# A fifth Strassen pair in the gate and up blocks of an encoder layer, and weights streamed from one array in load order

## The chip, the cores and the metric

The kernel runs on one core of one Trainium2 chip. TensorE (PE) multiplies into PSUM banks; VectorE (DVE), ScalarE (ACT) and GpSimd (POOL) prepare its operands and take its results; SyncE (SP) issues the loads, and 16 DMA engines carry all transfers. The metric is the device time of one execution in microseconds, the median of three runs. A profile is one further execution with its own time. Everything is computed in float32; a product of full precision is made of three matmuls of a faster rounded format (fp32r), as told below.

## The reference, cut to what matters

One layer over 256 rows of width 2048. An input projection of 5120 columns feeds differential attention and a convolution group; both are concatenated and go through an output projection. The part that the change touches is the second half, a gated feed-forward network with 5632 hidden columns:

```
h  = h + einsum('bsm,md->bsd', mixed, w_out)
hn = rms_norm(h, norm2_g)
a  = einsum('bsd,df->bsf', hn, w_gate)
bu = einsum('bsd,df->bsf', hn, w_up)
h  = h + einsum('bsf,fd->bsd', silu(a) * bu, w_down)
```

All weights, some 51 million float32 numbers, are read once from memory.

## The kernel before, in words

*Chunks.* The work of TensorE is a list of chunks, built ahead and run in that order by `run_chunks` (line 411). An ordinary chunk, called a "two" here, is a piece of a weight matrix of two row blocks of 128 by 512 columns. Each is cut in two parts on the chip: `hi`, its rounding to fp32r (`round_chunk`, line 328, on ScalarE, written to tile `whi`), and `lo`, the residue (`split_chunk`, line 336, on VectorE, tile `wlo`). The activations are cut the same way. A product is then hi·hi + lo·hi + hi·lo: three matmuls with 512 columns for each row block and each of the two halves (m = 0, 1) of the 256 rows, 12 for a two.

*Residues by DMA.* For some twos (`by_dma`) ScalarE writes -raw to `wlo` (line 333) behind the rounding, and GpSimd issues a DMA that adds raw's rounding to it in place (line 334), so that VectorE has nothing to do for it. `BY_DMA`, `DOWN_BY_DMA` and `gate_up_block` choose which.

*Pairs.* The 256 rows are two halves, gate and up are two column blocks, and two row blocks of 128 of the weights can be taken together: a 2x2 by 2x2 product. A "pair" (kind `s`) computes it with seven products in place of eight (`PRODUCTS`), so 21 matmuls where four row blocks as twos (one two of gate, one of up) take 24. It costs sums: of the activations once (`make_forms`, line 985, before the first block; `make_down_forms`, line 939, for each down pass), and for each pair of the weights: `first_sums` (lines 1035 to 1037) makes four sums (tile `wt`) from the loaded four pieces (tile `wb`, three of which are also used as they are); `round_pair` and `split_pair` round all seven on ScalarE (lines 1030 and 1052, tile `wh`) and take seven residues on VectorE (line 1059, tiles `wlb` and `wlt`).

*Blocks.* The feed-forward network has 11 blocks of 512 gate and 512 up columns (j = 0 to 10), in groups of 4, 4 and 3, each group followed by a down pass of two blocks. A block's order is a string: `s` a pair, `g` a two of gate, `u` a two of up (`ORDER`, `ORDERS`). Before, a block has pairs for the row blocks 0 to 3 with 8 to 11, and four twos each of gate and up for the rest (`REST`, `TWOS`). Behind its last pair, `bank_sums` (line 1183) combines the banks on VectorE with six sums and calls `sums_aside` (line 1039), in which GpSimd makes the first sums of the next pair that is not yet rounded, if it is loaded; `products_done` applies silu on ScalarE (lines 1202 and 1203); `block_done` (line 1206) takes two sums and two products on VectorE after the block's last two; `transposed` (line 893) transposes the result on TensorE for the down pass. The operand sums of a down pass are made during the last blocks of its group, one step at a time (`lag`).

*What sets the order.* The engines' instructions are issued in one fixed order by this program. While chunk t is multiplied, the residues of chunk t+2 and the rounding of chunk t+3 are issued (`LO_AHEAD`, `HI_AHEAD`), and everything that hangs on a finished chunk is a generator that advances at each `resume()`, two to a two and four to a pair. Each engine takes its own instructions strictly in that order, and a wait holds all behind it. `whi` and `wlo` have three buffers, `wh`, `wlb`, `wlt` and `wb` two, `wt` one, the loaded raw pieces `RAW_BUFS`; loads are issued on SP when a buffer is given up (`load_freed`).

*The passage to the network.* `out_done` (line 836) adds each quarter of the output projection to h, transposes it on TensorE (`ps_h`), scales it and cuts it, and sums its squares. The residual h is stored to memory (`hd`) by GpSimd's DMAs, and the down passes add to it there.

## Time and profile before

| | us |
|---|---|
| median of three runs (lowest, highest) | 1034.13 (1034.05, 1034.5) |
| the profiled execution, in all | 1035.56 |
| its span, first to last instruction | 1033.8 |
| TensorE busy | 1023.9 |
| VectorE busy | 906.9 |
| ScalarE busy | 668.0 |
| GpSimd busy | 179.6 |

The input projection with attention and convolution takes the first 247 us or so, the output projection goes to 338.7, where the first chunk of the feed-forward network starts, and the network fills the rest. The granted clock of TensorE was 1.00 in all windows shown. Matmuls are pipelined: a row gives 0.39 us for a single one, but the next starts before it ends, so that start to start is the cost that counts; for VectorE too, an instruction's row is a little longer than the step to the next one. A row of the timeline holds the start, the length, the engine, the line, the operation, output and inputs, shapes and the count, and in brackets the idle time before it with what ended it.

### The profile page before, as it was taken

What the parts mean: (1) busy time and instruction counts of PE and PEld (TensorE: products, weight loads), DVE (VectorE), ACT (ScalarE), POOL (GpSimd) and SP (SyncE); (2) the same over time, 40 slices, a digit from 0 to 9 for tenths busy, and PEclk for the clock granted to TensorE, in tenths of its full rate; (3) what the DMA queues carried; (4) which work ended last, traced back from release to release, by engine and by line L of the source; (5) the groups of instructions that cost most, each with busy time, mean ns of one, the idle gap of its engine ahead of it and who ended that gap; (6) DMA issues with size and microseconds to landing.
All of it is one profiled execution on the core that took longest, in us unless ns stands there. A gap on an engine that the chain in (4) does not pass through costs nothing.

```text
span 1033.8 us, 13146 instructions
## 1 busy us (share of the span) xinstructions
PE 1023.9 (99%) x4628; PEld 846.3 (82%) x4628; DVE 906.9 (88%) x1163; ACT 668.0 (65%) x863; POOL 179.6 (17%) x190
## 2 busy tenths in 40 slices
PE   9999999999999899999999999999999999999998
PEld 7888888888888688888888888888888888888887
DVE  6899999999756999899988897889989888789897
ACT  7644656665756576777756657677777556767662
POOL 0300112110000100212203222123022231220320
PEclk9999999999999999999999999999999999999999
DMA  9757554445458767987989898889798989797776
GB/s 339 248 198 260 187 184 164 160 167 171 164 175 278 221 220 218 285 261 210 255 256 230 292 276 252 254 240 240 245 280 236 260 231 302 228 259 229 234 190 176
DMA packets 116738, 239.71 MB, mean 232 GB/s; under 512 B 7872, under 2 KB 9152, under 8 KB 116672
## 3 DMA queue, kind: packets, MB, share of 16 engines
q1 hardware_dynamic: 105216, 203.58, 58.7%
q0 software_dynamic: 11168, 35.13, 18.1%
q8 instruction: 36, 0.59, 0.2%
q14 instruction: 30, 0.25, 0.1%
q10 hardware_dynamic: 288, 0.16, 0.1%
HBM read 204.24 MB, written 9.44 MB: 207 GB/s over the span
## 4 chain that ended last, share of the span: by engine, by line
PE 92%; DMA 3%; DVE 2%; issue 2%; ACT 0%; SPq 0%; POOL 0%; DVEq 0%; POOLq 0%; ACTq 0%
PE q L1102 11%; PE q L1096 11%; PE q L1097 11%; PE q L1077 9%; PE q L1076 9%; PE q L1075 9%; PE acc L369 9%; PE acc L370 9%; PE acc L375 9%; DMA wlo<-raw 2%; PE ps_a L903 1%; DVE wlo L339 1%; DMA raw<-in_w_in_dram 1%; PE ps_s L726 1%; PE ps_o L796 1%
## 5 line engine op out<-in xcount | busy, mean ns | idle before, releaser
L330 ACT CAST whi<-raw 128x1024 fp32r<-128x1024 f32 (+1 forms) x248 | 257.4, 1044 | 192.1 <-issue 87.5
L339 DVE TENSOR_TENSOR wlo<-raw,whi 128x1024 fp32r<-128x1024 f32 (+1 forms) x198 | 238.4, 1211 | 47.1 <-ACT whi L330 42.8
L1059 DVE TENSOR_TENSOR wlt<-wt,wh 128x1024 fp32r<-128x1024 f32 x130 | 153.1, 1219 | 16.4 <-ACT wh L1052 16.4
L1052 ACT CAST wh<-wt 128x1024 fp32r<-128x1024 f32 x130 | 132.6, 1051 | 36.2 <-DVE wt L1035 24.3
L1096 PE MATMUL q<-whi,chi 128*128 128x512 f32 x352 | 137.8, 391 | 0.0
L1097 PE MATMUL q<-whi,clo 128*128 128x512 f32 x352 | 137.0, 389 | 0.0
L1059 DVE TENSOR_TENSOR wlb<-wb,wh 128x1536 fp32r<-128x1536 f32 x65 | 113.9, 1753 | 16.2 <-ACT wh L1030 16.2
L334 POOL DMA_DIRECT2D wlo<-raw x50 | 43.6, 871 | 484.3 <-ACT wlo L333 313.9
L369 PE MATMUL acc<-whi,xhi 128*128 128x512 f32 x312 | 124.1, 398 | 0.0
L370 PE MATMUL acc<-whi,xlo 128*128 128x512 f32 x312 | 122.0, 391 | 0.0
L1075 PE MATMUL q<-wh,fhi 128*128 128x512 f32 x308 | 120.6, 392 | 0.0
L1076 PE MATMUL q<-wh,flo 128*128 128x512 f32 x308 | 119.9, 389 | 0.0
L1030 ACT CAST wh<-wb 128x1536 fp32r<-128x1536 f32 x65 | 95.8, 1473 | 8.9 <-PE q L1076 3.3
L586 DVE SCALAR_TENSOR_TENSOR y<-upad,cw,y 128x256 f32<-128x256 f32 x240 | 100.9, 480 | 0.0
L1102 PE MATMUL q<-wlo,chi 128*128 128x512 f32 x352 | 94.6, 390 | 3.2 <-DMA wlo<-raw 2.5
L375 PE MATMUL acc<-wlo,xhi 128*128 128x512 f32 x312 | 85.0, 393 | 0.0
L1102 PEld LDWEIGHTS q<-wlo,chi 128*128 128x128 f32 x352 | 65.8, 188 | 17.9 <-DMA wlo<-raw 3.5
L1096 PEld LDWEIGHTS q<-whi,chi 128*128 128x128 f32 x352 | 66.1, 188 | 13.6
L1097 PEld LDWEIGHTS q<-whi,clo 128*128 128x128 f32 x352 | 66.1, 188 | 13.5
L1096 PE MATMUL q<-whi,ahi 128*128 128x512 f32 x182 | 71.0, 390 | 0.0
L1097 PE MATMUL q<-whi,alo 128*128 128x512 f32 x182 | 70.8, 389 | 0.0
L1077 PE MATMUL q<-wlt,fhi 128*128 128x512 f32 x176 | 68.6, 390 | 0.2 <-DVE wlt L1059 0.2
(247 smaller groups left out, 1844.4 us busy)
## 6 DMA issues: line engine op xcount, KB each, us to landing
raw<-in_w_in_dram SPq DMA_DIRECT2D x78, 512.0 KB, 4.7
wlo<-raw POOLq DMA_DIRECT2D x50, 512.0 KB, 6.3
raw<-in_w_down_dram SPq DMA_DIRECT2D x46, 512.0 KB, 6.2
wb<-in_w_up_dram SPq DMA_DIRECT2D x44, 512.0 KB, 4.4
wb<-in_w_gate_dram SPq DMA_DIRECT2D x44, 512.0 KB, 5.5
raw<-in_w_gate_dram SPq DMA_DIRECT2D x44, 512.0 KB, 5.3
raw<-in_w_up_dram SPq DMA_DIRECT2D x44, 512.0 KB, 5.5
wb<-in_w_down_dram SPq DMA_DIRECT2D x42, 512.0 KB, 5.8
```

Source lines behind the costliest of these rows:

```text
L330: act.copy(c["hi"], c["raw"])
L339: dve.tensor_tensor(c["lo"], c["raw"], c["hi"].bitcast(F32), ALU.subtract)
L369: pe.matmul(ps[m], xhi[:, ms], hi[:, j, :], start=c["first"] and j == 0, stop=False)
L370: pe.matmul(ps[m], xlo[:, ms], hi[:, j, :], start=False, stop=False)
L375: pe.matmul(ps[m], xhi[:, ms], lo[:, j, :], start=False, stop=c["last"] and j == nk - 1)
L1059: dve.tensor_tensor(lo, raw, h.bitcast(F32), ALU.subtract)
L1075: pe.matmul(ps, hi, c["hi"][:, w], start=bool(first), stop=False)
L1076: pe.matmul(ps, lo, c["hi"][:, w], start=False, stop=False)
L1077: pe.matmul(ps, hi, c["lo"][w], start=False, stop=bool(last))
L1096: pe.matmul(ps, xs[i][0][:, ms], hi[:, i, :], start=i == 0 and bool(c["first"].get(qs[m])), stop=False)
L1097: pe.matmul(ps, xs[i][1][:, ms], hi[:, i, :], start=False, stop=False)
L1102: pe.matmul(sum_bank(c, qs[m]), xs[i][0][:, ms], lo[:, i, :], start=False, stop=i == 1 and bool(c["last"].get(qs[m])))
```

## The change

The weights are concatenated by the host into one flat array, in the order of the loads (`Stream`): each load takes the next piece, laid out with a partition's data side by side. A two's load is then a run of 4 KB for each of the 128 partitions (2 x 2 KB before), a pair's is one DMA with runs of 8 KB (two DMAs, 4 x 2 KB before).

Blocks 1 to 10 get a fifth pair, of the row blocks 4 and 5, in place of one two of gate and one of up; the rest is three twos each. Block 0 keeps four pairs, so the rows 4 and 5 are prepared in both forms. The orders become shorter, `sgsgsgsusuu` in place of `sggsggsuusuu`. The twos whose residue goes by DMA are others: gate's second and third and up's first and second (before: gate's first and second, up's second and fourth); in block 1 gate's third and up's first two; in the first block of the second and third group up's first two alone; in the down passes of four blocks, gate's third and fourth for the first and second.

The very first pair's sums go from VectorE to GpSimd and are issued six chunks ahead in place of three, and its loads nine ahead in place of seven. In `out_done` the sums of squares of the last quarter come behind the transposes, its store stays ahead. The operand forms get 640 columns in place of 512 each. The raw buffers go from five to four, with a fifth that lives until the network starts.

```
-RAW_BUFS = 5
+RAW_BUFS = 4
...
-NS = 4
-REST = [k for k in range(KD) if k % HK >= NS]
+PAIRS = [(0, 8), (1, 9), (2, 10), (3, 11), (4, 5)]
+NS = len(PAIRS)
+REST = [k for k in range(KD) if not any(k in p for p in PAIRS)]
 TWOS = [tuple(REST[i : i + 2]) for i in range(0, len(REST), 2)]
-BY_DMA = dict(g=TWOS[:2], u=TWOS[1::2])
-
-ORDER = "sggsggsuusuu"
-ORDERS = {0: "gugusgsgssuu", 1: "gsggsgsuusuu"}
+BY_DMA = dict(g=TWOS[1:], u=TWOS[:2])
+
+ORDER = "sgsgsgsusuu"
+ORDERS = {1: "gsgsgssusuu"}
+
+NS0 = 4
+TWOS0 = [*PAIRS[NS0:], *TWOS]
+ORDER0 = "gugusgsgssuu"
+DOWN_ORDER = "sggsggsuusuu"
...
-DORDERS = {4: (ORDER, ORDER), 3: ("gguusggsuu", "gsgsgsuuu")}
+DORDERS = {4: (DOWN_ORDER, DOWN_ORDER), 3: ("gguusggsuu", "gsgsgsuuu")}
 HD_LAG = 3
-DOWN_BY_DMA = {4: (dict(g=(0, 1), u=(1,)),) * 2, 3: (dict(g=(), u=()), dict(g=(0, 1), u=()))}
+DOWN_BY_DMA = {4: (dict(g=(2, 3), u=(1,)),) * 2, 3: (dict(g=(), u=()), dict(g=(0, 1), u=()))}
...
-PAIRS_AHEAD, SUMS_AHEAD = 7, 3
+PAIRS_AHEAD, SUMS_AHEAD = 9, 6
...
+class Stream:
...
+    def take(self, parts):
+
+        n = P * sum(w for *_, w in parts)
+        self.parts.append(parts)
+        self.at += n
+        return self.ap[self.at - n : self.at].rearrange("(p n) -> p n", p=P)
...
-            sp.dma_start(out=c["raw"][:, :, o : o + n], in_=rows[:, c["rows"], col : col + n])
-            o += n
+        sp.dma_start(out=c["raw"].rearrange("p k n -> p (k n)"),
+                     in_=stream.take([(c["w"], k, col, n) for k in c["ks"] for col, n in c["cols"]]))
...
             if t == first - SUMS_AHEAD:
-                first_sums(chunks[pairs[0]], dve)
+                first_sums(chunks[pairs[0]], pool)
...
         if n == D // N - 1:
-            h_squares(n, cs)
-            yield
-            yield
-            ss = small.tile([P, NM], F32, tag="ssh", name="ssh")
...
+            h_store(cs)
+            yield
+        yield
...
+        h_squares(n, cs)
         if n < D // N - 1:
-            h_squares(n, cs)
+            h_store(cs)
...
-        for i, kind in enumerate("ug"):
-            w, col = c["from"][kind]
-            sp.dma_start(out=c["b"][:, 2 * i : 2 * i + 2, :],
-                         in_=w.rearrange("(k p) n -> p k n", p=P)[:, c["rows"], col : col + N])
+        sp.dma_start(out=c["b"].rearrange("p a n -> p (a n)"),
+                     in_=stream.take([(c["from"][i][0], k, c["from"][i][1], N) for i in "ug" for k in c["ks"]]))
...
-                   BY_DMA if j > 1 and j not in FIRSTS else dict(g=(), u=BY_DMA["u"]) if j else
-                   dict(g=TWOS[2:3], u=TWOS[2:3]), swap=not j)
+                   dict(BY_DMA, g=TWOS[2:]) if j == 1 else BY_DMA if j > 1 and j not in FIRSTS else dict(BY_DMA, g=()) if j else
+                   dict(g=TWOS0[2:3], u=TWOS0[2:3]), swap=not j)
...
+    for c in [c for c in chunks if not c.get("spare_raw")][RAW_BUFS :: RAW_BUFS + 1]:
+        c["kept_raw"] = True
```

More of the change, by code (lines that the diff above doesn't have):

```diff
@@ L310, in block @@
                                first=part[0] == ks[0] and first, last=last and i == len(ks),
-                               done=done if i == len(ks) else None, spare=spare, by_dma=False,
-                               rows=slice(part[0], part[-1] + 1), load=load_chunk, round=round_chunk,
+                               done=done if i == len(ks) else None, spare=spare, by_dma=False, load=load_chunk, round=round_chunk,
                                split=split_chunk, multiply=multiply))
@@ L317, in load_chunk @@
         c["view"] = view
-        if c.get("spare_raw"):
+        if c.get("kept_raw"):
+            c["raw"] = view(keep.tile([P, NK * N], F32, tag="raw", name="raw"))
+        elif c.get("spare_raw"):
             c["raw"] = view(early.tile([P, 4 * N], F32, tag="wb", name="raw")[:, : NK * N])
@@ L414, in run_chunks @@
         pairs = [k for k in range(n) if chunks[k].get("kind") == "s"]
-        raws = [k for k in range(n) if chunks[k].get("kind") != "s" and not chunks[k].get("spare_raw")]
+        raws = [k for k in range(n) if chunks[k].get("kind") != "s" and not (chunks[k].get("spare_raw") or chunks[k].get("kept_raw"))]
         loaded, split = set(), set()
@@ L829, in tile_block, with h_store @@
     rstd2 = [rstd2s[:, m : m + 1] for m in range(NM)]
+    def h_store(cs):
+        for m in range(NM):
+            pool.dma_start(out=hd[m][:, cs], in_=h[m][:, cs])
     def h_squares(n, cs):
@@ L864, in out_done @@
                     pe.transpose(pt[:, i, m * P : (m + 1) * P], h[m][:, (k + i) * P : (k + i + 1) * P], ident)
-            if k % HK < NS:
-                rows = ffn["rows"][:, k // HK, k % HK : k % HK + 2, :]
+            if k not in REST:
                 for i in range(2):
-                    act.activation(rows[:, i, :], pt[:, i, :], AF.Copy, scale=col("g2", k + i))
-            else:
-                a = REST.index(k)
-                hi, lo = (ffn[x][:, a : a + 2, :] for x in ("chi", "clo"))
+                    p, half = next((p, pair.index(k + i)) for p, pair in enumerate(PAIRS) if k + i in pair)
+                    act.activation(ffn["rows"][:, half, p, :], pt[:, i, :], AF.Copy, scale=col("g2", k + i))
+            if k in REST or k in PAIRS[NS0]:
+                a = REST.index(k) if k in REST else 0
+                hi, lo = (ffn[x][:, a : a + 2, :] for x in ("chi", "clo")) if k in REST else lhs_two("h", k)
                 for i in range(2):
@@ L884, in out_done @@
         if n == D // N - 1:
+            yield
+            ss = small.tile([P, NM], F32, tag="ssh", name="ssh")
+            for m in range(NM):
+                dve.tensor_reduce(ss[:, m : m + 1], ss2[m], AX.X, ALU.add)
+            rsqrt_mean(rstd2s, ss, D, EPS)
             keepstack.close()
@@ L991, in make_forms @@
         flo = fp.tile([P, 7, NS, P], F32R, tag="flo", name="flo")
-        f = fp.tile([P, 7, NS, P], F32, tag="wh", name="sums", bufs=2)
-        dve.scalar_tensor_tensor(f[:, 4], a21, -1.0, a22, ALU.mult, ALU.subtract)
-        dve.scalar_tensor_tensor(f[:, 5], f[:, 4], -1.0, a11, ALU.mult, ALU.subtract)
+        f = dict(zip((2, 4, 5, 6), range(4)))
+        f_ = fp.tile([P, 4, NS, P], F32, tag="wh", name="sums", bufs=2)
+        f = {form: f_[:, i] for form, i in f.items()}
+        dve.scalar_tensor_tensor(f[4], a21, -1.0, a22, ALU.mult, ALU.subtract)
+        dve.scalar_tensor_tensor(f[5], f[4], -1.0, a11, ALU.mult, ALU.subtract)
         act.copy(fhi[:, 0], a11)
@@ L1068, in multiply_pair @@
     def multiply_pair(c):
-        while (fs := c["pairs"]()) is None or len(plain) < len(REST):
+        while (fs := c["pairs"]()) is None or len(plain) < len(REST) + 2 * (NS - NS0):
             resume()
@@ L1137, in fast_block @@
             what = left[kind].pop(0)
-            c = dict(kind=kind, sums=sums, swap=swap, done=None, first={}, last={}, rows=what["rows"], **operands)
+            c = dict(kind=kind, sums=sums, swap=swap, done=None, first={}, last={}, ks=what["ks"], **operands)
             if kind == "s":
@@ L1157, in gate_up_block @@
     def gate_up_block(j):
-        fast_block(ORDERS.get(j, ORDER), [dict(p=p, rows=slice(p, p + HK + 1, HK)) for p in range(NS)],
-                   [dict(ks=ks, rows=slice(ks[0], ks[1] + 1, ks[1] - ks[0]), k=ks) for ks in TWOS],
+        fast_block(ORDERS.get(j, ORDER) if j else ORDER0,
+                   [dict(p=p, ks=k) for p, k in enumerate(PAIRS[: NS if j else NS0])],
+                   [dict(ks=ks, k=ks) for ks in (TWOS if j else TWOS0)],
                    dict(g=(w_gate, j * N), u=(w_up, j * N)),
@@ L1174, in down_pass @@
             end = {}
-            fast_block(order, [dict(p=p, rows=slice(k0 + p, k0 + p + HD + 1, HD)) for p in range(nd)], twos,
+            fast_block(order, [dict(p=p, ks=(k0 + p, k0 + p + HD)) for p in range(nd)], twos,
                        dict(g=(w_down, n * N), u=(w_down, (n + 1) * N)),
@@ L1363 @@
     given["rope"] = rope_constants()
+    weights = {name: given.pop(name) for name in WEIGHTS}
+    flat = nc.dram_tensor("in_weights_dram", (sum(w.size for w in weights.values()),), F32, kind="ExternalInput")
+    args.append(stream := Stream(flat.ap()))
     for name, a in given.items():
```

36 lines of the change are left out of this document (19 added, 17 removed).

## The prediction

> **What bounds the kernel now.** The page comes first: how full is each engine, and what does the chain that ended last consist of?
>
> ```profile
> span 1033.8 us, 13146 instructions
> PE 1023.9 (99%) x4628; PEld 846.3 (82%) x4628; DVE 906.9 (88%) x1163; ACT 668.0 (65%) x863; POOL 179.6 (17%) x190
> PE 92%; DMA 3%; DVE 2%; issue 2%; ACT 0%; SPq 0%; POOL 0%; DVEq 0%; POOLq 0%; ACTq 0%
> ```
>
> TensorE holds 92% of the chain, and VectorE is its next busiest neighbour. Second, the waits of TensorE; these are three of its six rows, and all six together are under 6 us:
>
> ```profile
> PE q L1102 <- DMA wlo<-raw: 2.5, 1, 2.5
> PE ps_h L864 <- DVE h L845: 0.8, 2, 0.5
> PE q L1102 <- DVE wlo L339: 0.5, 1, 0.5
> ```
>
> So TensorE sets the time by the number of its matmuls. Third, the pace of them, from the chain in order of time in block 5 of gate and up (each row is the last third, four matmuls, of a "two"):
>
> ```profile
> 662.94 0.91 PE q L1102 x4
> 665.66 0.91 PE q L1102 x4
> 673.14 0.91 PE q L1102 x4
> 675.86 0.91 PE q L1102 x4
> ```
>
> Two neighbouring twos (12 matmuls each) are 2.72 us apart: 0.2267 us a matmul. Between the second and third row lies a pair as well: 7.48 - 2.72 = 4.76 us for its 21 matmuls, again 0.2267. No waiting is left in this pace.
>
> Fourth, how much room VectorE has, in windows of one block each (columns: length, then busy time of PE, PEld, DVE, ACT, POOL). The first three are blocks 1, 2, 3, the next three 5, 6, 7, the last two 9 and 10; each window starts a few us after its block.
>
> ```profile
> 390.95:432.70 41.75, 41.75 (x192) 34.58 (x191) 38.58 (x40) 28.71 (x30) 8.43 (x7) 1.00 0.87 244
> 432.70:474.45 41.75, 41.75 (x192) 34.58 (x190) 37.56 (x40) 32.27 (x37) 8.77 (x7) 1.00 0.86 249
> 474.45:516.20 41.75, 41.61 (x187) 34.16 (x186) 39.53 (x45) 32.15 (x35) 8.63 (x7) 1.00 0.85 244
> 639.95:681.70 41.75, 41.75 (x191) 34.58 (x190) 34.40 (x35) 29.14 (x31) 8.45 (x7) 1.00 0.88 254
> 681.70:723.45 41.75, 41.75 (x191) 34.58 (x190) 37.55 (x40) 32.26 (x37) 8.79 (x7) 1.00 0.87 246
> 723.45:765.20 41.75, 41.75 (x189) 34.59 (x188) 39.53 (x45) 32.13 (x35) 8.61 (x7) 1.00 0.87 250
> 888.55:930.30 41.75, 41.75 (x191) 34.58 (x190) 35.09 (x36) 29.62 (x32) 8.44 (x7) 1.00 0.87 250
> 930.30:972.00 41.70, 41.70 (x189) 34.54 (x188) 37.05 (x45) 29.35 (x36) 9.36 (x5) 1.00 0.74 227
> ```
>
> VectorE is already busy for 34 to 40 us of a block's 41.75. That is the number on which this prediction turns.
>
> **The matmuls removed.** A block of gate and up has 4 pairs and 8 twos: 4x21 + 8x12 = 180 matmuls. With a fifth pair for two of the twos it has 5x21 + 6x12 = 177. Block 0 keeps four pairs, ten blocks change: 30 matmuls at 0.2267 = **-6.8 us**; a block shrinks from 41.75 to 41.07. Both bounds are close, as no row between shows another pace: -6.8 to -6.9.
>
> **VectorE's new work.** What pairs and twos cost there, start to start, from its timeline in block 6:
>
> ```profile
> 685.84 2.36 DVE L339 TENSOR_TENSOR wlo<-raw,whi 128x1024 fp32r<-128x1024 f32 x2
> 688.12 1.22 DVE L1035 TENSOR_TENSOR wt<-wb 128x1024 f32<-128x1024 f32 x1
> 689.37 0.69 DVE L1036 TENSOR_TENSOR wt<-wb,wt 128x512 f32<-128x512 f32 x1
> 690.10 0.69 DVE L1037 TENSOR_TENSOR wt<-wt,wb 128x512 f32<-128x512 f32 x1
> 690.71 1.75 DVE L1059 TENSOR_TENSOR wlb<-wb,wh 128x1536 fp32r<-128x1536 f32 x1
> 692.38 2.35 DVE L1059 TENSOR_TENSOR wlt<-wt,wh 128x1024 fp32r<-128x1024 f32 x2
> 694.65 1.22 DVE L339 TENSOR_TENSOR wlo<-raw,whi 128x1024 fp32r<-128x1024 f32 x1
> ```
>
> A residue of a two takes (688.12 - 685.84)/2 = 1.14. A pair takes 690.71 - 688.12 = 2.59 for its sums and 694.65 - 690.71 = 3.94 for its residues, 6.53 together. GpSimd still takes the sums of at most one pair a block, since it is called once, behind the bank sums; so the fifth pair falls on VectorE whole. From block 2 on, four twos' residues still go by DMA in an ordinary block, which leaves two on VectorE where there were four: 6.53 - 2x1.14 = +4.25 a block. Block 1 goes from six on VectorE to three: 6.53 - 3x1.14 = +3.11. Against 41.07 (the last window 41.02):
>
> block 1: 41.69, over by 0.6; block 2: 41.81, over by 0.7; block 3: 43.78, over by 2.7; block 5: 38.65, 2.4 spare; block 6: 41.80, over by 0.7; block 7: 43.78, over by 2.7; block 9: 39.34, 1.7 spare; block 10: 41.30, over by 0.3. In 2-3, 6-7 and 10 the excess is the operand sums of the coming down pass, unchanged and in the same places.
>
> An excess is a stall only where VectorE's lead is used up. The lead is small at the second pair of a block, as the two sums that end a block wait for its last two:
>
> ```profile
> 676.35 1.29 DVE L1211 TENSOR_TENSOR sum<-q,sum 128x512 f32<-128x512 f32 x2 [1.77 <-PE q L1102]
> 677.55 1.29 DVE L1216 TENSOR_TENSOR sum<-sum,sum 128x512 f32<-128x512 f32 x2
> ```
>
> They take 2.5 and start some 0.4 after TensorE ends the block; 3.94 of residues follow: ready at 6.8. In the new order (pair, two, pair) TensorE needs them after 4.76 + 2.72, some 0.45 of transposes and two matmuls: 8.4. That is 1.6 of lead. From there a pair with a two by DMA gives back 7.48 - 6.53 = 0.95, less what the down pass's sums take. Blocks 6 and 7: 3.4 over, against 1.6 of lead and a down pass of unchanged order that takes up the tail; I put 0.5. Blocks 1 to 3: 4.1 over, starting behind block 0, in which VectorE was never ahead, and with two pairs side by side in block 1's order (6.53 of work in 4.76); I put 2.6. Block 10: 0.4. Together **+3.5**. Bounds: 0, if the lead holds everywhere; 0.6 + 0.7 + 2.7 + 0.7 + 2.7 + 0.3 = 7.7, if there is none. The value is near the middle. ScalarE gains per block no more than the elements VectorE does (under 4 us) and is idle for 9.4 or more in every window: no term. If VectorE is late, its next users are ScalarE's roundings of the sums and, behind these in ScalarE's queue, the copies that start an accumulating DMA.
>
> **Where the stages meet.** Block 0 starts while VectorE does the operand forms, the first pair's sums and the last rows of h (VectorE's rows, then, in the second fence, those of TensorE that waited):
>
> ```profile
> 337.30 1.22 DVE L1035 TENSOR_TENSOR wt<-wb 128x1024 f32<-128x1024 f32 x1
> 338.56 0.69 DVE L1036 TENSOR_TENSOR wt<-wb,wt 128x512 f32<-128x512 f32 x1
> 339.28 0.69 DVE L1037 TENSOR_TENSOR wt<-wt,wb 128x512 f32<-128x512 f32 x1
> 339.89 2.35 DVE L339 TENSOR_TENSOR wlo<-raw,whi 128x1024 fp32r<-128x1024 f32 x2
> 342.16 1.28 DVE L845 TENSOR_TENSOR h<-h,acc 128x512 f32<-128x512 f32 x2
> ```
>
> ```profile
> 341.17 1.20 PE L1102 MATMUL q<-wlo,chi 128*128 128x512 f32 x4 [0.52 <-DVE wlo L339]
> 342.90 0.33 PE L864 MATMUL ps_h<-ident,h 128*128 128x128 f32 x1 [0.54 <-DVE h L845]
> 362.34 1.20 PE L1102 MATMUL q<-wlo,chi 128*128 128x512 f32 x4 [2.54 <-DMA wlo<-raw]
> ```
>
> The sums (337.30 to 339.89) go to GpSimd, six chunks earlier. The forms get a quarter longer; behind the last pause that is one operation of 1536 columns and two of 512, by the wlb row (1.67 for 1536) +0.42 and twice +0.14, 0.7. So VectorE is 1.9 earlier at 339.89 and 342.16, and the waits of 0.8 and 0.5 on it go: **-1.3**. Bounds: 0, if GpSimd's sums come late, and -3.8, if the wait of 2.54 goes too; I leave that one, because the copies that start its DMA come behind the same work of ScalarE. The squares that move behind the transposes hold nobody: the reciprocal root is used only at block 0's end.
>
> GpSimd's sums have a neighbour there, and the row of their time is wide:
>
> ```profile
> L1035 POOL TENSOR_TENSOR wt<-wb x14: 2404/2734/5328, 422.0 to 956.3; 128x1024 f32<-128x1024 f32 x14
> ```
>
> At worst the first operation takes 5.3 instead of 2.7, still inside the six chunks, 16 us, that it has. The Trainium skill (SBUF — State Buffer, on the shared port pair) says that a VectorE instruction with two inputs in SBUF and a GpSimd one that reads SBUF exclude each other. By that the sums would stand against the residues and the forms just then, which speaks against this part of the change; the row's spread is of that kind, and the sum stays as it is by the one and by the other.
>
> **The DMAs.** Loads move the same bytes; runs of 4 and 8 KB for 2 KB make fewer packets. The rows: the page's queue of the loads; the group of the copies that start a residue by DMA; block 5's last activation; and, of the accumulating DMA's line, the time from issue to landing:
>
> ```profile
> q1 hardware_dynamic: 105216, 203.58, 58.7%
> L333 ACT ACTIVATE wlo<-raw 128x1024 fp32r<-128x1024 f32 x50 | 52.7, 1054 | 0.0
> 677.24 0.72 ACT L1203 ACTIVATE sum<-sum,rstd 128x512 f32<-128x512 f32 x1
> DMA to landing us min/median/max: 4.8/6.3/10.6
> ```
>
> The loads are hidden now (no wait of TensorE names one) and stay so: 0, with a gain in landings at most. What may not stay hidden is a residue by DMA. In the new order the first of a block is prepared behind the activations that end at 677.96, 6.8 after the last pair (its end is 671.2, 8 matmuls before the row 673.14, less 0.16), then two roundings, rounding and negation at 1.05 each and the issue at 0.9: landed at 6.8 + 4.2 + 0.9 + 6.3 = 18.2 at the latest. TensorE needs it after two twos, pair, transposes, two, pair and 8 matmuls: 5.44 + 4.76 + 0.45 + 2.72 + 4.76 + 1.8 = 19.9. A slack of 1.7 holds a median landing and not a long one. I put **+0.8** for the few long ones; bounds 0 and the rival below.
>
> **The sum.** -6.8 - 1.3 + 3.5 + 0.8 = -3.8. The profiled execution took 1035.56 us in all, 1.8 around its span, so it would take 1031.8; it lies 1.4 above the median of the runs, 1034.13, from which I subtract: **1030.3**.
>
> **The rivals.** (1) The lead holds everywhere, as in today's blocks, where VectorE at 39.5 of 41.75 delays nobody: -6.8 - 1.3 = 1026.0. Against it: the lead of 1.6 at every second pair. (2) VectorE becomes the bound in blocks 1-3, 6, 7 and 10: 7.7 in place of 3.5, and the fifth pair gives nothing: 1034.5. For it: the table of excesses; against it: the buffers of two chunks. (3) Slower: the residues by DMA come late. Today's load packets take 0.587x1033.8x16/105216 = 0.092 us each on an engine; at that pace a pair's 8 KB run takes 0.37. An accumulation has 128/16 = 8 rows on each engine; if each waits for one run's turn, that is 8x0.28 = 2.2 more, a median landing of 8.5. That is above the slack of 1.7 on 6.3, from where it decides; at a spread of some 1.5 I put 1.2 a block on its two early residues, in seven blocks 8.4, for the 0.8: 1030.3 + 7.6 = 1037.9. Against it: shorter queues. The Trainium skill (DMA: Bandwidth & Descriptors, on queues, rings and completion order) says that each DMA engine takes turns between queues a packet at a time, which is this mechanism; no run here shows how long a packet of these runs is. (4) The longer runs alone do nothing: part of every case.
>
> **How the numbers follow.** Chances: forecast 0.45 (own range 1028 to 1032.5), (1) 0.25, (2) 0.17, (3) 0.13. A measurement of this kernel tells about 0.2%, 2.1 us, from no change, so faster ends at 1032.1: 0.42 of the forecast, all of (1), a little of (2), 0.69; within: 0.03 + 0.12 + 0.02 = 0.17; slower 0.14. The range goes from 1024.8, (1) with half of the 2.5 us wait gone, to 1036.5, the lower half of (3).
>
> **What would show it.** Right: 30 of TensorE's 4628 instructions gone; windows of 41.1 in blocks 5 and 9 with VectorE near 38.7; waits of TensorE on wlt in blocks 1 to 3 of 2 to 3 us together; no wait on h or wlo near 340. Wrong: waits on wlt in block 5, or on wb (GpSimd taking fewer sums), or a median landing over 8 with waits on wlo.

## The result, and the profile after

The changed kernel takes 1042.89 us (median of 5 runs, 1041.88 to 1044.92), beside 1034.5 us for the kernel before on the same chip: a ratio of 1.0078 with a 95% interval of 1.0061 to 1.0094. It is slower, where 1030.3 was forecast, and outside the range that ended at 1036.5.

The page first: span, engines, the loads' queue, and the accumulating DMAs (count, size, median us from issue to landing).

```profile
span 1040.1 us, 12940 instructions
PE 1021.8 (98%) x4598; PEld 839.4 (81%) x4598; DVE 953.8 (92%) x1199; ACT 690.1 (66%) x876; POOL 193.6 (19%) x194
q1 hardware_dynamic: 46800, 203.57, 55.8%
wlo<-raw POOLq DMA_DIRECT2D x51, 512.0 KB, 9.0
```

The 30 matmuls are gone (4598 for 4628), and yet the span is 6.3 us longer. VectorE has 46.9 us more to do. The loads move the same bytes in 46800 packets, and the accumulating DMAs, 6.3 us in the median before, need 9.0. Then TensorE's waits (total us, times, longest):

```profile
PE q L1130 <- DMA wlo<-raw: 8.9, 12, 1.6
PE q L1105 <- DVE wlt L1087: 2.8, 3, 1.6
...
PE acc L400 <- DVE wlo L364: 1.1, 1, 1.1
```

There was one wait on a residue by DMA; there are twelve. Those on `wlt`, the sums' residues, are near the forecast. Windows of exactly one block each, from first matmul to first matmul, for blocks 1, 2, 3, then 5, 6, 7, then 9, 10 (length, then busy time of PE, PEld, DVE, ACT, POOL, and at the end the granted clock, the share of the DMA engines and their GB/s):

```profile
383.04:427.32 44.28, 41.97 (x186) 33.78 (x185) 43.70 (x46) 29.92 (x30) 6.16 (x5) 1.00 0.74 235
427.32:469.25 41.93, 41.40 (x186) 33.94 (x185) 41.45 (x45) 34.24 (x37) 10.41 (x9) 1.00 0.85 253
469.25:512.79 43.54, 41.88 (x187) 33.78 (x185) 43.16 (x48) 30.99 (x35) 7.87 (x7) 1.00 0.75 213
636.89:677.96 41.07, 41.07 (x186) 34.02 (x185) 39.96 (x41) 32.58 (x34) 10.05 (x8) 1.00 0.87 261
677.96:719.03 41.07, 41.07 (x187) 34.02 (x185) 40.12 (x43) 31.69 (x35) 7.91 (x7) 1.00 0.85 260
719.03:762.51 43.48, 41.81 (x187) 33.79 (x185) 43.10 (x47) 30.93 (x34) 7.80 (x7) 1.00 0.79 232
889.49:931.23 41.74, 41.37 (x187) 33.93 (x185) 39.98 (x41) 31.95 (x34) 9.15 (x8) 1.00 0.87 262
931.23:972.77 41.54, 41.37 (x187) 33.93 (x185) 41.16 (x44) 28.19 (x35) 9.04 (x7) 1.00 0.82 238
```

Blocks 5 and 6 have the forecast's 41.07. In blocks 1, 2, 3, 7 and 10 VectorE is busy for all but 0.4 to 0.6 us, which suggests that it sets the pace there; the experiments test it. Block 0 went the other way, here in the kernel before and then after:

```profile
338.67:385.84 47.17, 43.11 (x189) 34.28 (x188) 44.25 (x49) 30.97 (x37) 3.82 (x6) 1.00 0.75 234
```

```profile
339.75:383.04 43.29, 42.39 (x189) 34.42 (x188) 41.18 (x46) 30.36 (x37) 5.41 (x6) 1.00 0.77 254
```

It starts 1.08 us later and is 3.88 shorter. All of the 6.3 us can be placed by the starts of the blocks in both traces (the listed waits come to less, since the shortest stalls are not listed as waits): matmuls -6.8; passage and block 0 -2.8; blocks 1 to 10 over their own matmuls +11.0 (block 1 3.2, block 2 0.9, block 3 2.0 beyond the 0.4 it had, block 7 2.4, block 8 1.4, blocks 9 and 10 1.1); down passes +4.9.

Why a block waits is seen in block 3. VectorE, ScalarE, GpSimd and TensorE after the change, one fence each (start, length, and in brackets the idle time before with what ended it):

```profile
477.27 0.68 DVE L995 TENSOR_TENSOR dlo<-raw_act,dhi 128x512 fp32r<-128x512 f32 x1
477.87 1.21 DVE L1063 TENSOR_TENSOR wt<-wb 128x1024 f32<-128x1024 f32 x1
...
480.45 0.68 DVE L948 TENSOR_TENSOR alo<-ps_a,ahi 128x512 fp32r<-128x512 f32 x1
...
485.59 1.22 DVE L1063 TENSOR_TENSOR wt<-wb 128x1024 f32<-128x1024 f32 x1
```

```profile
479.11 1.06 ACT L1080 CAST wh<-wt 128x1024 fp32r<-128x1024 f32 x1 [2.31 <-DVE wt L1063]
480.56 1.05 ACT L1080 CAST wh<-wt 128x1024 fp32r<-128x1024 f32 x1 [0.40 <-DVE wt L1065]
481.52 1.04 ACT L355 CAST whi<-raw 128x1024 fp32r<-128x1024 f32 x1
482.47 1.06 ACT L358 ACTIVATE wlo<-raw 128x1024 fp32r<-128x1024 f32 x1
```

```profile
483.89 0.89 POOL L359 DMA_DIRECT2D wlo<-raw  x1 [8.23 <-ACT wlo L358]
```

```profile
493.09 1.20 PE L1130 MATMUL q<-wlo,chi 128*128 128x512 f32 x4 [1.20 <-DMA wlo<-raw]
```

From one pair to the next VectorE takes 485.59 - 477.87 = 7.72 us, where TensorE needs 7.48: a pair's 6.53 and two residues of the down pass's operands (`alo`, and a `dlo` like the one at 477.27). It idles for less than 0.1 us. ScalarE waits 2.31 for its sums, and behind that wait stand the rounding and the negation of the next two, whose end releases the accumulating DMA: issued at 483.89, landed 9.2 later, and TensorE, there since 491.9, waits 1.20. So a late VectorE can show up as a late DMA; that it does so here is tested below.

### The profile page after: what moved, and what is told of

Same layout as the page of the kernel before. It is cut to its first block, busy times and chain, and to the rows that moved or that the text cites. A ratio compares the mean times of both kernels' runs of the same rounds, so it can differ in the third digit from the quotient of the medians.

```text
span 1040.1 us, 12940 instructions
## 1 busy us (share of the span) xinstructions
PE 1021.8 (98%) x4598; PEld 839.4 (81%) x4598; DVE 953.8 (92%) x1199; ACT 690.1 (66%) x876; POOL 193.6 (19%) x194
## 3 DMA queue, kind: packets, MB, share of 16 engines
q1 hardware_dynamic: 46800, 203.57, 55.8%
## 5 line engine op out<-in xcount | busy, mean ns | idle before, releaser
L1080 ACT CAST wh<-wt 128x1024 fp32r<-128x1024 f32 x150 | 155.3, 1051 | 84.8 <-DVE wt L1063 55.8
L1087 DVE TENSOR_TENSOR wlt<-wt,wh 128x1024 fp32r<-128x1024 f32 x150 | 176.4, 1216 | 0.0
L1103 PE MATMUL q<-wh,fhi 128*128 128x512 f32 x378 | 147.3, 390 | 0.0
L1104 PE MATMUL q<-wh,flo 128*128 128x512 f32 x378 | 147.2, 389 | 0.0
L1087 DVE TENSOR_TENSOR wlb<-wb,wh 128x1536 fp32r<-128x1536 f32 x75 | 131.2, 1750 | 10.7 <-ACT wh L1058 10.4
L1124 PE MATMUL q<-whi,chi 128*128 128x512 f32 x264 | 104.2, 395 | 0.0
L1125 PE MATMUL q<-whi,clo 128*128 128x512 f32 x264 | 102.8, 389 | 0.0
L1104 PEld LDWEIGHTS q<-wh,flo 128*128 128x128 f32 x378 | 71.0, 188 | 14.9
L1103 PEld LDWEIGHTS q<-wh,fhi 128*128 128x128 f32 x378 | 71.0, 188 | 14.6
L1130 PE MATMUL q<-wlo,chi 128*128 128x512 f32 x264 | 71.8, 394 | 5.9 <-DMA wlo<-raw 5.9
L1063 DVE TENSOR_TENSOR wt<-wb 128x1024 f32<-128x1024 f32 x60 | 73.1, 1219 | 0.8
```

Of the source, the lines that this page charges most:

```text
L1080: act.copy(hi[:, i : i + 2], t[:, i : i + 2])
L1087: dve.tensor_tensor(lo, raw, h.bitcast(F32), ALU.subtract)
L1103: pe.matmul(ps, hi, c["hi"][:, w], start=bool(first), stop=False)
L1104: pe.matmul(ps, lo, c["hi"][:, w], start=False, stop=False)
L1124: pe.matmul(ps, xs[i][0][:, ms], hi[:, i, :], start=i == 0 and bool(c["first"].get(qs[m])), stop=False)
L1125: pe.matmul(ps, xs[i][1][:, ms], hi[:, i, :], start=False, stop=False)
```

## The experiments

Theory 1: the long runs of the loads delay the accumulating DMAs (rival 3 of the prediction). Theory 2, in the first expectations: the denser order of pairs and calls delays them; it was then split in two. Theory 3: the loads of the pairs beside them delay them, whatever their runs. Theory 4: VectorE is late by itself. Theory 5, formed later: VectorE's lateness gets to TensorE through ScalarE and the DMA. Other numbers are explained in the expectations that use them. Ratios are to the kernel before, measured on the same chip beside it, with a 95% interval.

**How long the runs are.** `e1_short_runs` is the changed kernel with runs of 2 KB as before; `e3_short_pairs` has them for the pairs alone, `e4_runs_1k` has 1 KB in the network; `e2_long_runs_only` is the kernel before with the flat array.

```
 class Stream: take()
-  rearrange("(p n) -> p n", p=P)
+  rearrange("(k p n) -> p k n", k=len(parts), p=P)     # e1; e3: for pairs; e4: halves of 256 columns
```

> The changed kernel, its loads in the same order from the same flat array, but each row block's 128x512 piece laid out by itself, so that a load moves runs of 2 KB as before the change. Theory 1 (the long runs hold each turn of a DMA engine longer, so the accumulating DMAs land late): their median landing goes from 9.0 back to 6.3 to 7 us, TensorE's waits on wlo<-raw from 8.9 us to under 2, the time to 1031 to 1035 (the waits of VectorE's own in blocks 0 to 3, some 3 us, stay). Theory 2 (the denser order of pairs, the other twos and the calls that lie closer together delay them): landing stays at 8.5 or more, time 1040 to 1044.

> The kernel before with nothing changed but the flat array: runs of 4 KB for a two, one DMA with runs of 8 KB for a pair; four pairs a block as before. Theory 1: median landing of the accumulating DMAs from 6.3 to 8.5 or 9.5 us, waits of TensorE on them in the down passes and at block ends (where the slack before was 1.5 to 3 us), time up by 3 to 7 us, 1037 to 1042. Theory 2: landing 6 to 6.5, time within 1.5 us of the kernel before.

> The changed kernel with runs of 2 KB for the pairs alone (one DMA of 1 MB as in the change), the twos stay at 4 KB. Theory 1, if the length of a turn counts: most of the loads' bytes at 8 KB are now at 2, so landing 6.5 to 7.5 us, time 1033 to 1037. Theory 2: no difference to the changed kernel, 1040 to 1044.

> The changed kernel with runs of 1 KB for all loads of the feed-forward network (the projections' at 2 KB). Theory 1 gives a dose: landing at or below that with 2 KB, 5.5 to 6.5 us, and a time at or below it unless the loads themselves, whose packets are less efficient, come late (waits on raw or wb would show that). Theory 2: 1040 or more.

Measured: e1 1056.37 us, 1.0189 [1.0158, 1.0219]; e3 1050.63, 1.0142 [1.0119, 1.0165]; e4 1053.37, 1.0167 [1.0149, 1.0185]; e2 1034.94, 0.9997 [0.9982, 1.0011]. From e1's page (a group's busy time and mean ns, then its idle time; then the DMAs):

```profile
L1063 DVE TENSOR_TENSOR wt<-wb 128x1024 f32<-128x1024 f32 x60 | 73.3, 1221 | 19.3 <-DMA wb<-in_weights_dram 18.5
...
wlo<-raw POOLq DMA_DIRECT2D x51, 512.0 KB, 8.9
```

Theory 1 falls: with 2 KB the accumulating DMAs need 8.9 us, with 1 KB 8.5, with 8 KB 9.0, and in e2 the long runs leave them at 6.1, where the kernel before has 6.3. On the rule of the Trainium skill that the prediction cites (DMA: Bandwidth & Descriptors, queues, rings and completion order; turns by packets): an effect of the run's length on another queue's landing is not seen here between 1 and 8 KB. What short runs do is make the pairs themselves late (VectorE waits 18.5 us for `wb` in e1, 0.8 for everything there after the change). The times of e1, e3 and e4 lie above what either theory expected, for that reason. The fifth pair needs the long runs; the kernel before gains nothing from them.

**Where the residues by DMA are.** `e5_down_dma_back` undoes an edit to the down passes that the prediction gave no term.

```
-DOWN_BY_DMA = {4: (dict(g=(2, 3), u=(1,)),) * 2, ...
+DOWN_BY_DMA = {4: (dict(g=(0, 1), u=(1,)),) * 2, ...
```

> The changed kernel with the down passes' residues by DMA where they were before (gate's first and second two, not its third and fourth); all else as changed. In the changed kernel's trace the four down passes of the first two groups are 4.4 us longer in all than before (41.99, 41.99, 42.62, 42.87 for 41.76, 40.80, 41.74, 40.80) with waits on wlo<-raw behind accumulating DMAs that took 10 to 14 us beside the stores of the residual. Theory 3 (what counts is which DMAs stand beside an accumulating one): 3 to 5 us less than the changed kernel, 1038 to 1040, landings in the down passes 5 to 9. Theory 4 (VectorE behind is what makes them late, wherever they are): less than 1.5 us.

Measured 1038.52 us, 1.0036 [1.0022, 1.0050], 4.4 less than the changed kernel. The down passes fall back to the length they had before, within 0.4 each. The edit costs 4 us. From the issue of a down pass's accumulating DMA to TensorE's need it is much the same in all three, 10.7 us in the mean in the changed kernel, 10.1 in e5 and 10.2 before; the landing is not: 10.2, 7.3 and 7.2. The latest ones stand behind the stores of the residual: in the first group's second pass, GpSimd issued four stores from 555.89 to 557.57, the last of which landed at 570.1, and the DMA issued at 559.43 landed at 572.6, 13.1 later. In e5 that pass's first two were issued ahead of the stores, at 549.67 and 555.66, and landed in 5.8 and 7.5.

`e6_no_dma` takes no residue by DMA in blocks 1 to 10, and `e8_sums_first` lets VectorE take the residues of the sums (`wlt`) ahead of those of the loaded pieces (`wlb`).

```
-                   dict(BY_DMA, g=TWOS[2:]) if j == 1 else BY_DMA if j > 1 ...
+                   dict(g=TWOS0[2:3], u=TWOS0[2:3]) if not j else dict(g=(), u=()), swap=not j)     # e6
-        rest(lob, b[:, 1:], hi[:, SUMMED:])                          # e8: the same line behind the loop
```

> The changed kernel with no residue by DMA in blocks 1 to 10 of gate and up; VectorE takes all of them, 1.14 us each (35 of them). It measures whether VectorE's demand as the prediction counted it is right. Ordinary blocks then ask 43.2 to 48.3 us of VectorE for 41.07 of matmuls; the sum of the excesses over all ten blocks is some 39 us, so 1055 to 1068 us with VectorE busy without a pause in the blocks and no wait on wlo<-raw there. If VectorE's lead and buffers cover more than counted: under 1048.

> The changed kernel with the residues of a pair in another order: those of the four sums (wlt) first, those of the three plain pieces (wlb) last. The first products use wlt only, the first wlb is used by the fifth product, so the pair may start 1.7 us earlier against VectorE; and a pair's load, which waits for wlb, is issued some 2.3 us later, behind the accumulating DMA rather than ahead of it. Theory 3: median landing of the accumulating DMAs from 9.0 to 6.5 to 7.5 us, waits on wlt gone, 1032 to 1038. Theory 4: landings stay near 9, at most the 3 to 4 us of waits on wlt go, 1039 or more. In both, waits on wb may come up, since it lands later.

Measured: e6 1078.81 us (a single run), 35.9 more than the changed kernel and more than expected, with 10.2 us of waits on `wlt` in 15 places. The 35 residues that VectorE takes over, at 1.14 us, are 39.9. The two numbers are near each other in part by luck: some 8.5 of the 35.9 are five stretches at half the clock (see the last section), and blocks 4, 5 and 8 take 40.12, 41.32 and 40.12 us with all their residues on VectorE, 40.12, 41.07 and 41.49 in the changed kernel. So VectorE had room in those three; in blocks 2, 3, 6, 7 and 10, where a down pass's sums are made, it had none. e8 1056.35, 1.0211 [1.0191, 1.0231]: the median landing fell to 6.9, as Theory 3 said, but the waits on `wlo` rose to 13.1 us. In the gate and up blocks the mean time from issue to need had fallen too, from 9.5 to 8.6 us. Landing alone doesn't set the time; the first sign that the issue matters too. Most of e8's loss lies in the down passes, 20.5 us over their length before, and is not traced further.

**Four pairs.** `e7_four_alternating` puts four pairs in the alternating order into the kernel before; `e9_four_pairs` is the changed kernel with four pairs in all blocks, and the old orders and residues by DMA.

```
-BY_DMA = dict(g=TWOS[:2], u=TWOS[1::2])     # e7, on the kernel before
+BY_DMA = dict(g=TWOS[1:3], u=TWOS[:2])
-ORDER = "sggsggsuusuu"
+ORDER = "sgsgsgsguuuu"
-PAIRS = [(0, 8), (1, 9), (2, 10), (3, 11), (4, 5)]      # e9, on the kernel after
+PAIRS = [(0, 8), (1, 9), (2, 10), (3, 11)]
-ORDER = "sgsgsgsusuu"
+ORDER = "sggsggsuusuu"
```

> The kernel before, four pairs and runs of 2 KB, with the order of a gate and up block made alternating (sgsgsgsguuuu for sggsggsuusuu from block 2 on) and the residues by DMA at gate's second and third and up's first and second two; VectorE's work is the same 34 to 39.5 us a block. Theory 3 (an alternating order issues each accumulating DMA one or two us behind a pair's load of 1 MB, and the two share the engines): median landing 8 to 9.5 us for those between pairs, 1.5 MB of loads or more beside each for the 1.0 before, and 1 to 4 us more time than before. Theory 4 (five pairs' demand on VectorE and the loads make them late): landing 6 to 7, time within 1 us of before.

> The changed kernel with four pairs in every block, and with the orders and the residues by DMA of the kernel before, the down passes among them. What is left of the change is the flat array with its long runs, GpSimd's first sums and the last output chunk's place. Theory 3 (the time was lost with the fifth pair: pair loads beside the accumulating DMAs make them land late): those landings are back at 6.0 to 6.5 us, the waits on wlo are under 2 us in all, and what remains is the gain at the passage into the network, 2.8 us by the blocks of the changed kernel less 1.1 us of the output projection: 1030.5 to 1033 us, under the kernel before. Rival (the loss lies in the parts beside the fifth pair, in GpSimd's sums or the passage): 1036 us or more, with waits of TensorE before 400 us.

e7 took 1059.73, 1.0236 [1.0202, 1.0269]; four twos of up in a row at the end of a block made other waits (TensorE on the sums, 3.0 us in 12 places), and its listed waits are far from the 25 us that it lost, so it tells little of the order. e9 took 1031.6 us, 0.9963 [0.9950, 0.9975]: faster than both kernels, by the passage alone. Its block 0 has 43.29 us as in the changed kernel, starts at 338.58 and not 339.75 (the longer operand forms belong to the fifth pair: VectorE comes to the residues behind them at 336.27, in the changed kernel at 337.44), and TensorE waits once in the network:

```profile
PE q L1105 <- DVE wlt L1087: 0.9, 1, 0.9
```

**The loads or VectorE.** `e10_no_pair_loads` leaves out the loads of the pairs in blocks 1 to 10 and uses old pair tiles; `e11_less_vector` leaves out half of the sums' residues there. Each leaves everything else.

```
+        if c["again"]:                                   # e10, in load_pair
...
+            c["b"] = held_b[-2]
...
+            return
-        for i in (2, 0):                                 # e11, in split_pair
+        for i in (2,) if c["less"] else (2, 0):
```

> The changed kernel; in the gate and up blocks 1 to 10 the weights of the pairs are not loaded, and the two pair tiles loaded last before them are used again. This leaves out 1 MB of loads for each of five pairs in ten blocks; every instruction of TensorE, VectorE and ScalarE stays, and the accumulating DMAs stay. Theory 3 (late because of the loads beside them): the accumulating DMAs of these blocks, 9.1 us in the mean before, land in 5.5 to 6.5 us, the waits on wlo fall from 8.9 us to under 3 us, and the time is 1031 to 1036 us; those of the down passes remain late. Theory 4 (VectorE hands the residue or the buffers on too late, the loads have no part): landings stay at 8.5 us or more, or the waits stay whatever the landings do, 1041 to 1044 us.

> The changed kernel; in the gate and up blocks 1 to 10 VectorE forms half of the residues of each pair's sums (the second instruction of the two, 1.14 us a pair, is left out), and the half that is there is used in the place of the other. All loads and all accumulating DMAs stay. Theory 4 (VectorE's lateness sets the waits): the waits on wlt and wlo both go, 1030 to 1034 us. Theory 3 (loads beside): the landings stay at 8.5 to 9.5 us; the waits on wlt go (2.8 us now), those on wlo fall only by what VectorE's earlier hand-over of the raw tile is worth, to 4 to 8 us from 8.9: 1036 to 1040 us.

Measured: e10 1041.19 us, 1.0056 [1.0036, 1.0076]; e11 1031.39, 0.9961 [0.9942, 0.9981]. The answer for the accumulating DMAs issued from 425 to 490 us (blocks 2 and 3) in the changed kernel, in e10 and in e11:

```profile
DMA to landing us min/median/max: 8.7/9.1/9.7
```

```profile
DMA to landing us min/median/max: 4.5/4.5/4.6
```

```profile
DMA to landing us min/median/max: 8.4/8.5/10.3
```

So Theory 3 is right about the landing: without the loads it halves. But the time fell only 1.7 us, not to 1031 to 1036. And e11, with landings as late as ever, lost all waits on `wlo` outside the down passes. These are the waits of e10 and of e11:

```profile
PE q L1138 <- DMA wlo<-raw: 7.9, 7, 2.2
PE q L1113 <- DVE wlt L1095: 2.9, 4, 1.6
```

```profile
PE q L1130 <- DMA wlo<-raw: 3.7, 2, 1.9
...
PE q L1105 <- DVE wlt L1087: 1.0, 1, 1.0
```

Of e10's seven waits on `wlo` four lie in down passes and three where the next stage's loads are beside; with the loads gone, blocks 1, 3 and 7 still take 43.56, 44.05 and 42.59 us. Both of e11's lie in down passes. Theory 4 is right about the time, but the totals say too little: the down passes, left as in the change, take 8.1 us over the kernel before in e10's trace and 7.2 in e11's, for 4.9 in the changed kernel, 1.7 and 3.4 of it at half the clock (last section). In the gate and up blocks e10 saved 3.5 us and e11 all of the 11.

**The way from VectorE to TensorE.** `e13_dma_first` changes ScalarE's order alone: the rounding and negation of a two by DMA stand ahead of the roundings of the pair before it. `e14_dma_first_down_back` adds e5. `e16_less_vector_down_back` is e11 with e5, `e17_no_loads_down_back` is e10 with e5.

```
+            if first < t and i < n and i < t + 1 + hi_lead and chunks[i]["by_dma"]:     # in run_chunks,
+                load(i)                                                                 # ahead of split_next
+                ...
+                chunks[i]["round"](chunks[i])
+                i += 1
```

> The changed kernel with one thing put earlier in ScalarE's order: the rounding and the negation of a two whose residue goes by DMA stand ahead of the roundings of the sums of the pair before it, not behind them. Theory 5 (VectorE's lateness reaches TensorE through ScalarE: ScalarE waits for VectorE's sums, 55.8 us in all in the changed kernel, and the copy that starts the accumulating DMA stands behind that wait): the DMAs are issued some 3 to 4.5 us earlier (two roundings of 1.05 us and a wait of 1.5 to 2.3), landings stay near 9, the waits on wlo in the gate and up blocks, some 6 of the 8.9 us, go, and the time is 1035 to 1039 us, 0.993 to 0.997 of the changed kernel. Rival (ScalarE has no part, or the earlier copy only waits for its load or its buffer and holds the pair's roundings up): waits on wlo of 7 us or more stay, or move to wlt, 1041 us or more.

> The same earlier place in ScalarE's order, with the down passes' residues by DMA where the kernel before has them. Theory 5 and the down passes' share together (4.4 us by the earlier run): 1031.5 to 1035 us, 0.997 to 1.0005 of the kernel before, with under 1 us of waits on wlo and some 3 us on wlt. Rival: as with the residues moved back alone, 1.003 to 1.005 of the kernel before.

> The changed kernel with the down passes' residues by DMA where the kernel before has them, and in the gate and up blocks 1 to 10 half of the residues of each pair's sums left out (the half that is there is used in the place of the other). If VectorE's lateness and the down passes' placement are the whole loss, no wait on wlo is left and the time is that of the forecast's first rival, 1025.5 to 1028 us, 0.991 to 0.994 of the kernel before. If a third cause is there (the granted clock, loads): 1029 us or more.

> The changed kernel with the down passes' residues by DMA where the kernel before has them, and without the loads of the pairs in the gate and up blocks 1 to 10 (the two pair tiles loaded last before them are used again, which leaves 1 MB a pair out). What VectorE costs by itself, when no accumulating DMA of these blocks is late: by the waits left in blocks 1, 3 and 7 without those loads (2.5, 3.0 and 1.5 us over a block's 41.07) 1031.5 to 1034.5 us. If VectorE has no part of its own: 1026 to 1028.5 us. If the loads have no part: 1037 to 1039 us.

Measured: e13 1040.99 us, 1.0066 [1.0049, 1.0083]; e14 1036.13, 1.0013 [1.0004, 1.0022], just over its range (in block 0 a wait of 2.9 us on `wlt`, as in e13, and 1.7 us lost at half the clock behind it); e16 1027.6, 0.9935 [0.9913, 0.9956]; e17 1034.27, 1.0000 [0.9990, 1.0011]. e13's waits, and the landings of 425 to 490 us:

```profile
PE q L1112 <- DVE wlt L1094: 5.9, 6, 2.9
PE q L1137 <- DMA wlo<-raw: 2.2, 2, 1.3
```

```profile
DMA to landing us min/median/max: 4.6/5.2/6.3
```

The waits on `wlo` in the gate and up blocks are gone (both that are left lie in down passes). Theory 5 holds for them. The expectation was wrong on two points: the landings fell as well, which fits Theory 3, since the earlier DMA is issued ahead of a pair's load and not just behind it; and the time fell by 1.9, not by 4 to 8, because the earlier copies held up the first pair of block 0 (the wait of 2.9) and VectorE's lateness came out at other places (`wlt`, the sums). For one and the same DMA, the second of block 3, from the starts in the traces (TensorE's need is the start of the two, and 8 matmuls, 1.81 us):

| kernel | from issue to TensorE's need | landing | room |
|---|---|---|---|
| after | 7.8 | 9.2 | -1.3 |
| e10, without the pairs' loads | 7.7 | 4.5 | 3.2 |
| e11, VectorE relieved | 9.8 | 9.2 | 0.6 |
| e13, earlier copies | 12.6 | 4.6 | 8.0 |

Either remedy alone frees this DMA. e16 and e17 put sizes to them, by spans of 1024.7 and 1032.6 beside 1036.4 in e5 (ratios 0.9935, 1.0000 and 1.0036). With VectorE relieved (897.6 us of work, where the kernel before has 906.9) and the loads in place, nearly nothing is lost: the span before less the matmuls' 6.8 and the passage's 2.8 is 1024.2. VectorE's extra work, with the pairs' loads left out, costs 7.9 us more (6.7 by the ratios), and the loads, on top of it, another 3.8 (3.7 by the ratios). So VectorE's work is the larger part, and the loads cost something only where VectorE is late.

**A version with all of it.** `e12_four_in_1` is e5 with four pairs in block 1; `e19_dma_first_1_to_9` is e14 with the earlier copies in blocks 1 to 9 alone; `e18_four_in_1_dma_first` has both.

```
-                   [dict(p=p, ks=k) for p, k in enumerate(PAIRS[: NS if j else NS0])],      # e12, e18
+                   [dict(p=p, ks=k) for p, k in enumerate(PAIRS[: NS if j > 1 else NS0])],
-            if first < t and ... and chunks[i]["by_dma"]:                                   # e18, e19
+            if first < t and ... and chunks[i].get("early"):
```

> The changed kernel with the down passes' residues by DMA where the kernel before has them, and with four pairs, not five, in block 1, in the order of the kernel before. Theory 3 with the sums' lateness in block 1 as my forecast had it (2.6 us in blocks 1 to 3): the waits on wlt fall from 3.0 to about 1 us, 2.5 us less than with the down passes' residues alone moved back, that is 0.9985 to 1.0020 of the kernel before. Rival (block 1's excess comes from the start of the network and not from its fifth pair): the time stays at 1.003 to 1.004 of the kernel before.

> The changed kernel with the down passes' residues by DMA where the kernel before has them and the earlier copies in blocks 1 to 9 alone, so that block 0 and the last block and pass keep their order. The earlier copies cost 2.9 us at the first pair of block 0 (one wait on wlt) and some 0.7 us between the last block and the last pass; without these two, 1031.5 to 1033.5 us, 0.996 to 0.999 of the kernel before. Rival (block 0's loss only moves into block 1): 1035 us or more.

> All that the runs point to, in one kernel: the change with the down passes' residues by DMA where the kernel before has them, four pairs in block 1, and in blocks 1 to 9 the copies that start an accumulating DMA ahead of the roundings of the pair's sums. If the waits on wlo (6.2 us in the kernel without the earlier copies, six of them) go and none on wlt comes in their place: 1029 to 1032 us, 0.995 to 0.998 of the kernel before. Rival (the earlier copies cost the sums of block 3 and 7 what they save): 1033.5 us or more, 0.999 and up.

Measured: e12 1035.08 us, 0.9999 [0.9989, 1.0009], as expected, with 41.75 us in block 1; e19 1034.06, 0.9991 [0.9980, 1.0002], between its two expectations; e18 1031.01, 0.9965 [0.9953, 0.9977], as expected. Blocks 1, 3 and 7 in e19:

```profile
383.18:426.70 43.52, 41.67 (x186) 33.87 (x185) 42.97 (x45) 29.11 (x30) 5.54 (x5) 1.00 0.74 242
467.78:510.22 42.44, 41.86 (x186) 33.86 (x185) 42.17 (x45) 32.83 (x37) 7.37 (x8) 1.00 0.77 238
716.30:757.99 41.69, 41.51 (x186) 33.87 (x185) 41.42 (x44) 32.39 (x36) 6.67 (x7) 1.00 0.80 243
```

VectorE is still full in them. With the way through the DMA made short and block 1's fifth pair taken out, e18 beats both kernels; but its ratio is that of e9, which has no fifth pair at all. It has 27 matmuls fewer than e9, worth 6.1 us; by the traces of the two, 3.8 of this goes in blocks 1 to 10 and the down passes and 1.4 at the passage with its longer forms. What the fifth pair saves is nearly all spent on the work that it brings.

## Why the prediction was wrong

Direction and time were wrong; rival 3 had the direction and the landing (8.5 forecast, 9.0 measured) with a mechanism that fell. By the steps of the sum:

- *The matmuls, -6.8*: right. 4598 instructions, 41.07 us in blocks 5 and 6.
- *Where the stages meet, -1.3, bounds 0 to -3.8*: -2.8 of its mechanism was there. The waits on h and on `wlo` near 341 went, and so did the wait of 2.54 that I had left in; the longer forms make a new one of 1.1 at 338.7 (TensorE after the change):

```profile
338.72 1.20 PE L400 MATMUL acc<-wlo,mchi 128*128 128x512 f32 x4 [1.10 <-DVE wlo L364]
```

- *VectorE's new work, +3.5, bounds 0 to 7.7*: mis-sized. The table of excesses was nearly right: it had 41.81, 43.78, 43.78 and 41.30 for blocks 2, 3, 7 and 10, which took 41.93, 43.54, 43.48 and 41.54. What failed is the discount for the lead: in 3 and 7 it was spent, and only block 6, with 41.07 for 41.80, was carried by it. Block 1 took 44.28 for the table's 41.69, and as e12 gives 41.75 with four pairs there, its fifth pair is the cause. Block 8, which the table leaves out, lost 1.4, with a wait of 1.1 on a late DMA. In e19, where hardly any DMA is late, the excesses of blocks 1 to 10 and of the down passes come to 7.6 us, so this term had the size of rival 2's 7.7. The places are others, so the agreement is in part luck: 2.5 in block 1 (0.6 in the table), 1.0 and 0.6 in blocks 3 and 7 (2.7 each), 2.7 in the down passes (none).
- *ScalarE "no term"*: the step that failed first. The prediction named the path (ScalarE's roundings of the sums and, behind these, the copies that start an accumulating DMA) and gave it no price, since ScalarE has idle time. Idle time was the wrong measure: it is spent waiting for VectorE at the head of an ordered queue, 55.8 us in all after the change (24.3 before; the kernel before stands first):

```profile
ACT wh L1052 <- DVE wt L1035: 24.3, 22, 4.2
```

```profile
ACT wh L1080 <- DVE wt L1063: 55.8, 39, 5.7
```

- *The residues by DMA, +0.8*: it should have been some 4.4 (e5's excess over blocks 1 to 10 and the down passes less e19's, which differs in ScalarE's order alone: 12.0 - 7.6; 1.7 of it is a stretch at half the clock behind a late one). The slack was worked out for the first DMA of a block, with ScalarE free and a landing of 6.3; the late ones were mostly the later ones, issued behind a late VectorE and landing in 9. That a landing depends on the load just ahead was not asked, though the new order puts most of these DMAs right behind the start of a pair's 1 MB.
- *The down passes*: no term, though the change moves their residues by DMA. It cost 4 us, by placing them behind the stores of the residual. An edit of one line was left out of the sum.

Together: -6.8 - 2.8 + 7.6 + 4.4 + 4 = 6.4, the span's +6.3. Of the signs named beforehand, a median landing over 8 with waits on `wlo` came true; there was no wait on `wlt` in block 5. VectorE was at 39.96 in block 5's window for the 38.7 forecast: one residue, at 675.77, took 2.21 us for 1.23 while GpSimd made its sums (from 674.22), and 0.4 us of another block's residue falls into the window. Left open is how e7's order would do without its four twos at the end.

## What to carry to other kernels

Before giving an engine more work, follow who waits for it in order, not only who reads its tiles: an engine that is "idle for 9 us a block" may hold, behind one wait, the copy that starts a transfer of 9 us, and then the lateness reaches the critical engine with another name on it. Price a small transfer by what is loaded beside it after the change, not by its median before, and take a row for every line of the diff. When the nearest engine is at 90% in every stage, trade work off the first one only in the stages where the second has room.

## What was not expected of the hardware

An accumulating DMA of 512 KB landed in 4.5 us with no pair's load beside it and in 9.1 with them, and the length of the loads' runs, 1 to 8 KB, made little difference to that (8.5 to 9.0). The records of its packets tell more: the one issued at 483.89, 1.1 us behind a pair's load that landed at 488.5, moved its first packet at 488.7, 4.8 us after its issue; in e13 the same one, issued 3.7 us ahead of the next pair's load, moved its first after 1.5 us. It is not simply that such a transfer waits for the end of a load that the other queue has begun. Of the eight of blocks 2 and 3 in the changed kernel, three moved their first packet after 4.2 to 4.8 us, but four after 2.1 to 3.4, while the load beside them landed 5.5 to 7.2 us after their issue (the eighth can't be told from the one before it). In e10 the six without a load beside them moved theirs after 1.4 us, with VectorE as busy as before, so VectorE's work isn't what holds them. The rule of turns by packets, which the Trainium skill states (DMA: Bandwidth & Descriptors, queues, rings and completion order), would let them start sooner; the packets' times alone don't show why they didn't.

The granted clock can fall after a short wait. In e10, TensorE waited 1.85 us and ran 1.3 us, and then 3.7 us at a granted clock of 0.54, with matmuls 0.43 us apart (timeline, then the window):

```profile
824.03 1.20 PE L1138 MATMUL q<-wlo,ahi 128*128 128x512 f32 x4 [1.85 <-DMA wlo<-raw]
...
825.72 0.63 PE L1132 MATMUL q<-whi,ahi 128*128 128x512 f32 x1
826.15 0.63 PE L1133 MATMUL q<-whi,alo 128*128 128x512 f32 x1
```

```profile
825.30:829.00 3.70, 3.70 (x11) 2.91 (x10) 1.28 (x1) 3.70 (x4) 0.86 (x1) 0.54 0.75 220
```

That doubles the price of the wait: such a stretch is 3.4 us at half the clock in the traces named here, 1.7 us lost. e5 has one behind a wait of 1.90 us in block 7, e11 two behind waits of 1.82 and 1.89, e6 five behind waits of 2.4 us and over; the changed kernel's own trace, with no wait in the network over 1.6, has none. The Trainium skill (TensorE: Matmul & The Clock Gate, Part 1) has the half clock follow an idle window of about 3.4 us, with 426.7 ns between matmuls of 512 columns: the pace agrees, the idle time here was shorter. A wait of 2.16 us at 571 us in e10 was not followed by a lower clock, and of the same wait of 2.5 us at 362 us in two kernels, one was (e2) and one was not (the kernel before), so what decides is not shown.
